# Modulation and first features of a hybrid attention layer: two hand-ordered stages replaced by one list schedule

## The chip, the cores and the metric

The kernel is one program on one core of a Trainium2 chip. The metric is the device time of one execution in microseconds (us). The engines are TensorE (PE in the profile, its weight loads PEld), VectorE (DVE), ScalarE (ACT), GpSimd (POOL) and SyncE (SP), which issues most DMAs.

## What is computed

One layer of a diffusion backbone: 512 latent and 256 context tokens, width 2048, two kinds of attention heads on one modulated input, one output projection, a gated MLP. The change concerns the first steps; the rest is named by its last lines:

```python
sc_, scc = jax.nn.silu(c), jax.nn.silu(c_ctx)                  # (1, 2048) each
mod_x = (sc_ @ w_ada[l] + b_ada[l])[:, None, :]                # six chunks of 2048
mod_c = (scc @ w_ada[l] + b_ada[l])[None, None, :]
sh1, s1, g1, sh2, s2, g2 = jnp.split(mod_x, N_MOD, axis=-1)
sh1c, s1c, ...           = jnp.split(mod_c, N_MOD, axis=-1)
h  = _modulate(_rmsnorm(x,  norm1_w[l]), sh1,  s1)             # h * (1 + scale) + shift
hc = _modulate(_rmsnorm(xc, norm1_w[l]), sh1c, s1c)
p  = h @ w_in                                                  # q, k, v, c_q, c_kv, k_rope
...
x = x + g1 * (_merge_heads(o_da, o_mla, ...) @ w_o[l])
h2 = _modulate(_rmsnorm(x, norm2_w[l]), sh2, s2)
x = x + g2 * _conv_ffn(h2, w_up[l], conv_w[l], conv_b[l], w_down[l])
return _rmsnorm(x, final_w)
```

## The kernel before

Everything is kept with features on the partitions: the 2048 model features are 16 tiles (index kt) of 128, each 512 latent columns (`a2k` tiles) and 256 context columns (two to a `c2k` tile). Products run on TensorE as three matmuls of split float32 numbers (helper `mm3`, L241 to L243): high x high, high x low, low x high, where ACT casts the high part and DVE subtracts it from the source to get the low part.

The program has five stages: modulation and first features; the other features and values; attention; output projection; MLP. The change rewrites the first.

**Head.** SP loads the rows `c` and `c_ctx`, then 16 tiles of x and 8 of ctx. ACT makes their silu; PE spreads each row over all partitions by matmuls with ones (L429), DVE copies `cb` and ACT copies `ccb` out of PSUM (L443, L445). ACT squares x (L435) and every other ctx tile (L437), DVE squares the other ctx tiles (L439) and adds all squares up (L441); PE sums over partitions (L448) and `rstd` makes the inverse norm (L297 to L302). GpSimd clears `cpad` and writes a DRAM tensor of zeros, `zero_d`, from it in pieces of 30 and of 18 floats (L333); attention reads it much later.

**Modulation of tile kt.** The scale needs 2048 products per feature for two vectors. For two tiles at once, `scales` loads four blocks `adak` of 512 KB, and PE multiplies them by `cpad` (which holds both silu vectors, 32 columns wide) in 16 matmuls per `products` call (L348, four for each block), accumulating into one PSUM bank `acc`; ACT copies the result (L350), PE sums it by `sel` (L352), DVE makes `a1` (L360). The shift reads a row block `ada` of 1 MB in two halves. For even kt DVE does it: four dot products of 1024 elements (L384; `modx` with `cb`, `modc` with `ccb`). For odd kt TensorE does it: 16 transposes in four batches (L400), each copied out by ACT (L401), then 16 products (L348) and a sum (L352).

**First features of tile kt.** DVE multiplies x by scale and inverse norm (L500, `h`), ACT adds the shift and rounds (L502), DVE makes the low part (L503); ACT and DVE split the weight block `w_g0` of 640 columns (L217, L218). PE then does five `mm3` of 512 columns and four of 256 into five latent and four context sums that stay in PSUM over all 16 tiles.

The head is written in the order wanted and kept by `manual_schedule`; from tile 0 on, `modulation(kt // 2 + 1)` is called ahead of every even kt and the framework's own scheduler orders the instructions by their place and by `high_priority`. Attention is ordered by a list scheduler in the kernel, class `Flow`: each step has an engine, a cost, a due time, and buffers taken from rings; a table `PLAN` shifts due times of parts, and `run` replays a queue per engine to fix the order. SP's loads are issued in order: one that waits for a free tile holds those behind it.

After the first stage `latent_norm` and `keys` read the sums out of PSUM, and ten more features follow, each with two weight blocks, while 48 more `ada` rows are multiplied by `cb` on DVE (helper `gemv`, L309).

Of the kernel before, what the change touches and what calls it, by code (L numbers as in the profile page):

```python
# [51 lines left out]
class Buf:  # L52


    def __init__(self, flow, ring, make):
        self.ring, self.make, self.tile = ring, make, None
        self.users, self.writers, self.readers, self.left = [], [], [], 0
# [7 lines left out]
class Step:  # L65
    __slots__ = ("eng", "cost", "lag", "at", "fn", "bufs", "left", "next", "takes", "start", "n", "ready")

    def __init__(self, eng, cost, lag, at, fn, n):
        self.eng, self.cost, self.lag, self.at, self.fn, self.n = eng, cost, lag, at, fn, n
        self.bufs, self.left, self.next, self.takes, self.ready = [], 0, [], [], 0.0  # L70
# [10 lines left out]


class Flow:
# [7 lines left out]
    def buf(self, make, ring=None, count=None):  # L91
        if ring and ring not in self.rings:
            self.rings[ring] = (count, [])
        return Buf(self, ring, make)

    def step(self, eng, cost, at, fn, r=(), w=(), needs=(), lag=None):
        at += self.plan.get(self.part, 0.0)
        s = Step(eng, cost, self.LAGS[eng] if lag is None else lag, at, fn, len(self.steps))
# [6 lines left out]
        for b in dict.fromkeys([*r, *w]):  # L105
            if b.ring and not b.users:
                s.takes.append(b)
            b.users.append(s)
            b.left += 1
            s.bufs.append(b)  # L110
# [10 lines left out]
    def run(self):  # L121
# [4 lines left out]
        engines = {"PE": -3.0, "ACT": 2.0, "DVE": 2.8, "POOL": 0.0, "SP": now, "X": -3.0}  # L126
# [6 lines left out]

        for s in self.steps:
            if not s.left:
                event(s.ready)
                open_[s.eng].append(s)
        order = []

        turns = {}  # L140
        for s in sorted(self.steps, key=lambda s: (s.at, s.n)):
            for b in s.takes:
                turns.setdefault(b.ring, []).append(b)

        def free(b):
            count, taken = self.rings[b.ring]
            if turns[b.ring][len(taken)] is not b:
                return False
            return len(taken) < count or taken[-count].left == 0

        event(now)
        for t in set(engines.values()):
            event(t)
        while events:
# [4 lines left out]
            for s in batch:  # L159
                if s is None:  # L160
                    continue
                for b in s.bufs:
                    b.left -= 1
                for n_ in s.next:
# [6 lines left out]
            for e in engines:  # L171
                while engines[e] <= now + 1e-9:
                    can = [s for s in open_[e] if s.ready <= now + 1e-9 and all(free(b) for b in s.takes)]
# [4 lines left out]
                    for b in s.takes:  # L178
                        self.rings[b.ring][1].append(b)
# [10 lines left out]
def layer_kernel(ctx: ExitStack, tc: tile.TileContext, small, rope, c_row, cc_row, x_t, ctx_t, ada, ada_k,  # L190
# [134 lines left out]


    zero_d = dram.tile([64, TT], F32, name="zero_d")
# [14 lines left out]
    def products(src, n):  # L342


        for j in range(4):
            for c in range(4):
                kt = 4 * j + c
                pe.matmul(acc[32 * c:32 * c + 32, :n], cpad[:, kt], src(kt), start=j == 0, stop=j == 3)  # L348
        row = st.tile([P, 2 * P], F32, tag="row", name=nm("row"), bufs=1)[:, :n]
        sc.copy(row, acc[:, :n])  # L350
        for i in range(n // P):
            pe.matmul(acc[:, 2 * i:2 * i + 2], row[:, i * P:(i + 1) * P], sel, start=True, stop=True)  # L352

    def scales(u, ws=None):

        ws = ws or columns(u)
        products(lambda kt: ws[kt // 4][:, kt % 4], 2 * P)
        for i in range(2):
            kt = 2 * u + i
            ve.tensor_scalar(out=a1[:, 2 * kt:2 * kt + 2], in0=acc[:, 2 * i:2 * i + 2], scalar1=b1[:, kt:kt + 1],  # L360
                             scalar2=col("n1", kt), op0=ALU.add, op1=ALU.mult)

    def columns(u):
        ws = []
        for j in range(4):
            wk = st.tile([P, 4, 2 * P], F32, tag="adak", name=nm("adak"), bufs=4)
# [91 lines left out]
    def modulation(u):  # L458
        if u:
            shifts(2 * u)  # L460
# [1397 lines left out]
```

## Time and profile before

| | us |
|---|---|
| median of three executions (2401.7 to 2403.73) | 2401.8 |
| the profiled execution, its own time | 2404.97 |
| its span in the trace | 2403.1 |
| PE busy in the span | 2342.3 (97%) |
| DVE busy | 1701.1 (71%) |
| ACT busy | 1153.6 (48%) |
| POOL busy | 336.3 (14%) |
| first matmul of the first features starts at | 49.30 |
| their last matmul starts at | 183.71 |

The trace gives, for each instruction, its start, its duration and what its engine waited for before it. Matmuls overlap, so the time that one takes on PE is the distance from its start to the next start, not its listed duration.

### The profile page before, as it was taken

The page shows a single profiled execution, that of the slowest core. Times are in us where ns is not written, and L with a number is a line of the kernel's source. Part 1 is how long each engine was busy: PE and PEld are TensorE (multiplying, and loading weights), DVE is VectorE, ACT ScalarE, POOL GpSimd, SP SyncE. Part 2 cuts the span into 40 slices and gives each one's busy share as a digit, 9 for nine tenths or more (in the row PEclk, how much of TensorE's full clock was granted, in tenths as well). Part 3 has the DMA queues.
Part 4 walks back from the last instruction along what each step waited for, and adds up shares of the span by engine and source line. Part 5 has one row for each costly group of instructions (what it writes and reads, how often), then busy time and mean ns, then how long its engine had stood idle before and what let it go on. Part 6 is the DMA issues. An engine that isn't in the chain of part 4 may idle for free.

```text
span 2403.1 us, 33008 instructions
## 1 busy us (share of the span) xinstructions
PE 2342.3 (97%) x12758; PEld 1981.3 (82%) x12758; DVE 1701.1 (71%) x2244; ACT 1153.6 (48%) x1752; POOL 336.3 (14%) x320
## 2 busy tenths in 40 slices
PE   5999999999999999999999999999999999999997
PEld 3678878887788888798888888888888888888887
DVE  6668886477878766399585757575767676766767
ACT  4333121177776732255454545454545444544546
POOL 0000000155433221100101010101010101111110
PEclk9999999999999999999999999999999999999999
DMA  8867899844521168333646465555554656565573
GB/s 281 295 230 277 304 336 330 269 130 139 156 64 50 34 255 320 131 115 97 144 130 144 128 144 137 140 140 141 132 147 123 153 122 158 123 153 128 140 186 105
DMA packets 132853, 404.31 MB, mean 168 GB/s; under 512 B 14628, under 2 KB 25380, under 8 KB 124244
## 3 DMA queue, kind: packets, MB, share of 16 engines
q1 hardware_dynamic: 106166, 351.66, 44.4%
q0 software_dynamic: 25376, 49.49, 11.9%
q8 instruction: 100, 1.64, 0.3%
q10 hardware_dynamic: 1152, 1.05, 0.1%
q14 instruction: 59, 0.48, 0.1%
HBM read 332.47 MB, written 69.67 MB: 167 GB/s over the span
## 4 chain that ended last, share of the span: by engine, by line
PE 84%; DVE 7%; DMA 4%; ACT 3%; issue 2%; SPq 0%; DVEq 0%; ACTq 0%
PE y L1577 12%; PE b L242 10%; PE b L241 10%; PE b L243 9%; PE z L1577 6%; PE y L1579 6%; PE s L241 3%; PE s L719 3%; PE s L243 3%; PE s L242 3%; PE z L1579 3%; DMA ada<-in_ada 3%; PE x L1577 2%; PE f L241 1%; PE f L242 1%
## 5 line engine op out<-in xcount | busy, mean ns | idle before, releaser
L1598 POOL DMA_DIRECT2D x_d<-xs x160 | 139.9, 1005 | 1161.4 <-ACT xs L1597 1159.5
L1433 DVE TENSOR_TENSOR wl<-wr,wh 128x1024 fp32r<-128x1024 f32 x144 | 176.5, 1225 | 158.6 <-ACT wh L1425 157.9
L1425 ACT CAST wh<-wr 128x1024 fp32r<-128x1024 f32 x144 | 151.1, 1049 | 234.8 <-PE b L242 120.7
L241 PE MATMUL b<-ah,wh 128*128 128x512 f32 (+1 forms) x664 | 256.8, 387 | 0.0
L242 PE MATMUL b<-al,wh 128*128 128x512 f32 (+1 forms) x664 | 256.7, 387 | 0.0
L243 PE MATMUL b<-ah,wl 128*128 128x512 f32 (+1 forms) x664 | 255.9, 385 | 0.0
L1433 DVE TENSOR_TENSOR wl<-rb,wh 128x1024 fp32r<-128x1024 f32 x123 | 150.0, 1220 | 126.8 <-ACT wh L1425 126.8
L1425 ACT CAST wh<-rb 128x1024 fp32r<-128x1024 f32 x123 | 129.3, 1051 | 186.5 <-PE b L242 115.8
L1433 DVE TENSOR_TENSOR wl<-ws,wh 128x1024 fp32r<-128x1024 f32 x123 | 150.1, 1221 | 89.8 <-ACT wh L1425 89.8
L1425 ACT CAST wh<-ws 128x1024 fp32r<-128x1024 f32 x123 | 128.3, 1043 | 130.1 <-PE b L242 45.2
L309 DVE CUSTOM_DVE_ANT_0 ada<-ada,cb,smt 128x2048 f32<-128x2048 f32 x64 | 152.3, 2383 | 46.6 <-DMA ada<-in_ada 46.6
L1577 PE MATMUL y<-a2k,wh 128*128 128x512 f32 x656 | 164.0, 392 | 0.0
L217 ACT CAST wh<-wr 128x1024 fp32r<-128x1024 f32 (+1 forms) x69 | 67.5, 978 | 195.2 <-PE s L243 48.8
L241 PE MATMUL b<-a2k,wh 128*128 128x512 f32 (+1 forms) x376 | 141.7, 377 | 5.9 <-ACT a2k L1282 4.3
L243 PEld LDWEIGHTS b<-ah,wl 128*128 128x128 f32 x664 | 124.8, 188 | 25.7
L241 PEld LDWEIGHTS b<-ah,wh 128*128 128x128 f32 x664 | 125.1, 188 | 22.9
L242 PEld LDWEIGHTS b<-al,wh 128*128 128x128 f32 x664 | 125.1, 188 | 22.0
L242 PE MATMUL b<-a2k,wh 128*128 128x512 f32 (+1 forms) x376 | 140.9, 375 | 0.0
L243 PE MATMUL b<-a2k,wl 128*128 128x512 f32 (+1 forms) x376 | 140.1, 373 | 0.0
L1577 PEld LDWEIGHTS y<-a2k,wh 128*128 128x128 f32 x656 | 118.6, 189 | 21.6
L218 DVE TENSOR_TENSOR wl<-wr,wh 128x1024 fp32r<-128x1024 f32 (+1 forms) x69 | 80.0, 1159 | 46.0 <-ACT wh L217 45.5
L722 DVE TENSOR_REDUCE m<-s 128x1 f32<-128x768 f32 x96 | 91.2, 951 | 28.0 <-PE s L719 27.5
(480 smaller groups left out, 5932.5 us busy)
## 6 DMA issues: line engine op xcount, KB each, us to landing
ada<-in_ada SPq DMA_DIRECT2D x64, 1024.0 KB, 7.0
rb<-in_w_up SPq DMA_DIRECT2D x123, 512.0 KB, 4.3
wr<-in_w_dn SPq DMA_DIRECT2D x88, 512.0 KB, 4.1
x_d<-xs POOLq DMA_DIRECT2D x160, 256.0 KB, 6.0
wr<-in_w_up SPq DMA_DIRECT2D x53, 512.0 KB, 4.2
wr<-in_w_f SPq DMA_DIRECT2D x34, 512.0 KB, 7.3
ada<-in_ada SPq DMA_DIRECT2D x32, 512.0 KB, 7.2
adak<-in_ada_k SPq DMA_DIRECT2D x32, 512.0 KB, 6.3
```

Source lines behind the costliest of these rows:

```text
L218: ve.tensor_tensor(dst_l, src, dst_h.bitcast(F32), op=ALU.subtract)
L241: pe.matmul(out, st[0], mv[0], start=start, stop=False, **kw)
L242: pe.matmul(out, st[0], mv[1], start=False, stop=False, **kw)
L243: pe.matmul(out, st[1], mv[0], start=False, stop=stop, **kw)
L309: ve.tensor_tensor_reduce(out=junk, in0=w, in1=vec, op0=ALU.mult, op1=ALU.add, scale=1.0, scalar=col("b_ada", j), accum_out=dst[:, j:j + 1])
L719: pe.matmul(s()[:, c0:c1], a, b[:, c0:c1], start=i == 0, stop=i == len(ms) - 1)
L722: step("DVE", 0.87, t + cost + 0.2, lambda: ve.tensor_reduce(out=m(), in_=s()[:, :TT], axis=AX.X, op=ALU.max, negate=True), r=[s], w=[m])
L1425: sc.copy(t, raw[:, k * n_:k * n_ + n_])
L1433: ve.tensor_tensor(t, raw[:, k * n_:k * n_ + n_], hi[k].bitcast(F32), op=ALU.subtract)
L1577: pe.matmul(o, w[j][0], hs[j], start=start and j == 0, stop=False, skip_group_check=True)
L1579: pe.matmul(o[:, h0], w[j][1], hs[j][:, h0], start=False, stop=j == 7, skip_group_check=True)
L1598: gp.dma_start(x1_d[dt], x, accum_op=ALU.add)
```

## The change

The first stage becomes part of a second `Flow`, and the `PLAN` table and the scheduler's rule for rings are replaced with it (a ring counts its live buffers instead of going round in turn, and a buffer taken early is not asked for again). This also reorders attention, whose code is otherwise the same.

Shifts: all tiles but 5 and 10 go to DVE, as dot products over a whole row of 2048 elements from one 1 MB load, 28 in place of 32 of half the length. Tiles 5 and 10 are turned on TensorE, with the products in two halves. The table of `ada` tiles in SBUF goes from five of 512 KB to three of 1 MB.

```diff
-        if kt % 2 == 0:
-            for i in range(2):
-                shift(kt, ws, i)
-            return
-        wt = st.tile([P, KT, P], F32, tag="wt", name=nm("wt"), bufs=1)
-        for q in range(4):
-            for i in range(4):
-                k = (q % 2) * 4 + i
-                pe.transpose(acc[:, i * P:(i + 1) * P], ws[q // 2][:, k * P:(k + 1) * P], ident)
-            sc.copy(wt[:, 4 * q:4 * q + 4].rearrange("p k f -> p (k f)"), acc)
-        products(lambda kt: wt[:, kt], P)
...
+    T0, PER = 31.0, 6.15
+    TURNED = (5, 10)
...
+            w = buf(lambda: st.tile([P, D], F32, tag="ada", name=nm("ada"), bufs=3), "ada", 3)
+            flow.part = f"lr{kt}"
+            load(T0 + PER * kt - 16 if kt else 16.9, 1060, lambda kt=kt, w=w: nc.sync.dma_start(w(), ada[kt]), [w])
...
+    def shift(kt):
+        if kt in TURNED:
+            turned_shift(kt)
+            return
+        w = rows[kt]
+        t = T0 + PER * kt - 10
+        for i in range(2):
+            at_b[i][kt] = b = buf(lambda: None)
+            d, vec = (modx, modc)[i][:, kt:kt + 1], (cb, ccb)[i]
+
+            def dot(d=d, vec=vec):
+                junk = st.tile([P, D], BF16, tag="junk", name=nm("junk"), bufs=1)
+                ve.tensor_tensor_reduce(out=junk, in0=w(), in1=vec, op0=ALU.mult, op1=ALU.add, scale=1.0,
+                                        scalar=col("b_ada", kt), accum_out=d)
+
+            flow.part = f"{'dp'[i]}{kt}"
+            step("DVE", 2.31, t + 2.6 * i, dot, r=[w, *wide[i]], w=[b], lag=0.2)
```

In the head, ACT now makes all squares and all copies of `cb` and `ccb`; the last two tiles' squares are not added on DVE but summed by PE (six matmuls of the sum over partitions in place of two); the inverse norm is made in two parts, latent and context.

```diff
-    for c0, c1, r in ((0, 480, slice(0, 64)), (480, TT, slice(64, P))):
-        gp.dma_start(zero_d[:, c0:c1].rearrange("p (k j) -> p k j", j=(c1 - c0) // KT),
-                     cpad[r, :, 2:2 + (c1 - c0) // KT])
...
+    z = kv.tile([P, TT], F32, tag="lt", name=nm("z"), bufs=3)[:64]
+    gp.memset(z, 0.0)
+    gp.dma_start(zero_d, z)
...
-            q = kv.tile([P, TT], F32, tag="nq", name=nm("nq"), bufs=1)
-            sc.square(q[:, :width], t)
...
+    for q, lat in zip(sq, lat0):
+        sc.square(q[:, :T], lat)
+    for t, lat in zip(ckv, lat0):
+        sc.copy(t[:, :T], lat)
```

So the zeros are written in the second stage, in whole rows, and the squares for the two latent norms are taken from PSUM ahead of the copies.

Three places in the order of the instructions. First TensorE in the middle of the stage, before, while an odd tile is turned (`ident` transposes of `ada`, products of `wt` with `cpad`; `b_332` to `s_426` are the feature sums):

```order
L243 MATMUL s_425<-a2k_1215,wl_986 128x512
L243 MATMUL b_332<-c2k_1213,wl_986 128x256
L241 MATMUL s_425<-a2k_1215,wh_985 128x512
L400 MATMUL b_334<-ident,ada_991 128x128 x4
L242 MATMUL s_425<-a2k_1216,wh_985 128x512
L243 MATMUL s_425<-a2k_1215,wl_986 128x512
L241 MATMUL b_332<-c2k_1213,wh_985 128x256
L242 MATMUL b_332<-c2k_1214,wh_985 128x256
L348 MATMUL b_334<-wt_993,cpad 32x128 x16
L243 MATMUL b_332<-c2k_1213,wl_986 128x256
L243 MATMUL s_426<-a2k_1215,wl_986 128x512
L242 MATMUL b_333<-c2k_1214,wh_985 128x256
```

The same engine in the changed program, between two tiles that are not turned (L252 to L254 are `mm3` now, L490 the scale products):

```order
L254 MATMUL b_475<-c2k_710,wl_589 128x256
L252 MATMUL s_450<-a2k_722,wh_692 128x512
L253 MATMUL s_450<-a2k_732,wh_692 128x512
L254 MATMUL s_450<-a2k_722,wl_708 128x512
L490 MATMUL b_346<-adak_756,cpad 32x256 x4
L490 MATMUL b_346<-adak_766,cpad 32x256 x4
L252 MATMUL b_475<-c2k_710,wh_579 128x256
L253 MATMUL b_475<-c2k_711,wh_579 128x256
L254 MATMUL b_475<-c2k_710,wl_589 128x256
L252 MATMUL b_457<-a2k_722,wh_692 128x512
```

Between the feature matmuls only the scale products are left; transposes stand there for two tiles instead of eight.

Second, VectorE in the middle of the stage, before (two weight blocks, then one even tile's four half dot products, each with its accumulator read; `modx`, `modc` without operands are those reads):

```order
L218 TENSOR_TENSOR wl_986<-wr_983,wh_985 128x640
L218 TENSOR_TENSOR wl_1038<-wr_1035,wh_1037 128x640
L384 ISA junk_1119,modx<-ada_1115,cb,smt 128x1024
L384 ISA modx 128x1
L384 ISA ada_1115,modc<-ada_1115,ccb,smt 128x1024
L384 ISA modc 128x1
L384 ISA junk_1121,modx<-ada_1117,cb,modx 128x1024
L384 ISA modx 128x1
L404 TENSOR_SCALAR modx<-b_334,smt 128x1
L404 TENSOR_SCALAR modc<-b_334,smt 128x1
```

And in the changed program (L557 the whole-row dot products, L581 and L586 the two passes over x):

```order
L557 ISA junk_964,modx<-ada_906,cb,smt 128x2048
L557 ISA modx 128x1
L581 SCALAR_TENSOR_TENSOR h_977<-a2k_232,a_91,rinv 128x512
L557 ISA junk_984,modc<-ada_906,ccb,smt 128x2048
L557 ISA modc 128x1
L586 SCALAR_TENSOR_TENSOR a2k_1008<-h_920,modx,a2k_979 128x512
L581 SCALAR_TENSOR_TENSOR h_920<-c2k_221,a_91,rinv 128x256
L557 ISA junk_1021,modc<-ada_966,ccb,smt 128x2048
L557 ISA modc 128x1
L478 TENSOR_TENSOR wl_1053<-wr_990,wh_1034 128x640
```

The dot products now stand singly between the passes over x of neighbouring tiles, twice as long each and for seven tiles of eight.

Third, SP at the end of the loads of x, before:

```order
L415 DMA a2k_205<-in_x_t 128x512
L418 DMA c2k_207<-in_ctx_t 128x512
L415 DMA a2k_209<-in_x_t 128x512
L375 DMA ada_211<-in_ada 128x1024
L375 DMA ada_213<-in_ada 128x1024
L367 DMA adak_215<-in_ada_k 128x1024
```

and in the changed program:

```order
L376 DMA a2k_257<-in_x_t 128x512
L463 DMA ada_263<-in_ada 128x2048
L463 DMA ada_278<-in_ada 128x2048
L463 DMA ada_290<-in_ada 128x2048
L376 DMA a2k_302<-in_x_t 128x512
L380 DMA c2k_307<-in_ctx_t 128x512
L376 DMA a2k_310<-in_x_t 128x512
```

Three whole `ada` rows (3 MB) moved ahead of the last two x tiles and the last ctx tile.

More of the change, by code (lines that the diff above doesn't have):

```diff
@@ L119, in step, with run @@
         return s
-    def run(self):
+    def run(self, begin):
         import heapq
         now = -100.0
-        engines = {"PE": -3.0, "ACT": 2.0, "DVE": 2.8, "POOL": 0.0, "SP": now, "X": -3.0}
+        engines = dict(begin)
         open_ = {e: [] for e in engines}
@@ L138, in run @@
         order = []
[L140 to L143, printed above, removed]
         def free(b):
[L146 to L153, printed above, removed]
+            return not b.ring or b.taken or turns[b.ring][0] is b and live[b.ring] < self.rings[b.ring]
         while events:
@@ L172, in run @@
                 while engines[e] <= now + 1e-9:
-                    can = [s for s in open_[e] if s.ready <= now + 1e-9 and all(free(b) for b in s.takes)]
+                    can = [s for s in open_[e] if s.ready <= now + 1e-9 and all(free(b) for b in s.bufs)]
                     if not can:
@@ L323, in layer_kernel @@
     st = tc.alloc_tile_pool(name="st", bufs=1, reuse_waits="tile")
-    zero_d = dram.tile([64, TT], F32, name="zero_d")
+    for i in range(4):
+        st.tile([P, 4, 2 * P], F32, tag="adak", name=nm("adak"), bufs=4)
+    st.tile([P, 640], F32, tag="wr", name=nm("wr"), bufs=2)
+    st.tile([P, D], F32, tag="ada", name=nm("ada"), bufs=3)
     cb = st.tile([P, D], F32, name="cb")
@@ L354, in scales @@
-    def scales(u, ws=None):
-        ws = ws or columns(u)
-        products(lambda kt: ws[kt // 4][:, kt % 4], 2 * P)
-        for i in range(2):
[L359 to L366, printed above, removed]
-            nc.sync.dma_start(wk, ada_k[u, j // 2][:, (j % 2) * 4:(j % 2) * 4 + 4])
-            ws.append(wk)
-        return ws
```

411 lines of the change are left out of this document (268 added, 143 removed), and 26 rows, old and new, of the table PLAN.

## The prediction

> **What bounds the kernel now.** I read the page first, then busy time in windows, the waits of PE in the first stage, and last its timeline start by start.
>
> ```profile
> PE 2342.3 (97%) x12758; PEld 1981.3 (82%) x12758; DVE 1701.1 (71%) x2244; ACT 1153.6 (48%) x1752; POOL 336.3 (14%) x320
> sum 200.00, PE 170.77 PEld 116.56 DVE 132.82 ACT 85.56 POOL 3.07; mean PE 8.54 PEld 5.83 DVE 6.64 ACT 4.28 POOL 0.15
> 100.00:110.00 10.00, 10.00 (x88) 8.10 (x88) 8.69 (x15) 5.27 (x10) 0.00 (x0) 1.00 0.71 244
> 110.00:120.00 10.00, 10.00 (x75) 6.56 (x74) 4.70 (x13) 2.85 (x5) 0.00 (x0) 1.00 0.99 358
> ...
> DMA packets 841, 1.54 MB, mean 384 GB/s; under 512 B 91, under 2 KB 91, under 8 KB 841
> ```
>
> The first row is the page's; the next three are windows (stretch, its length, busy time of PE, PEld, DVE, ACT, POOL, granted clock, DMA share, GB/s); the last is what the DMAs moved from 22 to 26 us. PE is idle for 2403.1 - 2342.3 = 60.8 us of the span, and 200 - 170.77 = 29.2 of that lies in the first 200 us, which the change rewrites. But in the middle of the stage PE is never idle, while DVE is idle 1.3 and 5.3 of 10 us and the DMAs move 244 to 358 GB/s, below the 384 they reached earlier. So two things can be had: PE's work in the middle, and the head, in which PE waits.
>
> ```profile
> PE s L448 <- DVE sqs L441: 14.0, 1, 14.0
> PE b L400 <- ACT wt L401: 1.4, 2, 0.7
> 49.30 1.22 PE L241 MATMUL s<-a2k,wh 128*128 128x512 f32 x2
> 183.71 0.39 PE L243 MATMUL b<-a2k,wl 128*128 128x512 f32 x1
> ```
>
> The waits (line, releaser, total us, times, longest) show the head's 14.0 us and little else. From the first feature matmul to the last start pass 134.4 us; with its 0.39 the stage ends at 184.1.
>
> **What is taken from PE.** Rows of PE's timeline (start, duration), one odd tile being turned and one block of scale products:
>
> ```profile
> 102.41 0.60 PE L400 MATMUL b<-ident,ada 128*128 128x128 f32 x4
> 102.76 0.48 PE L242 MATMUL b<-a2k,wh 128*128 128x512 f32 x1
> 103.08 0.39 PE L243 MATMUL b<-a2k,wl 128*128 128x512 f32 x1
> ...
> 107.72 1.08 PE L348 MATMUL b<-wt,cpad 128*32 128x128 f32 x32
> 108.73 0.39 PE L243 MATMUL b<-c2k,wl 128*128 128x256 f32 x1
> 108.95 0.39 PE L243 MATMUL s<-a2k,wl 128*128 128x512 f32 x1
> 109.18 0.28 PE L242 MATMUL b<-c2k,wh 128*128 128x256 f32 x1
> 109.30 0.32 PE L352 MATMUL b<-sel,row 128*128 128x2 f32 x2
> 109.48 0.37 PE L243 MATMUL b<-c2k,wl 128*128 128x256 f32 x1
> 109.69 0.40 PE L241 MATMUL s<-a2k,wh 128*128 128x512 f32 x1
> ...
> 114.22 0.64 PE L348 MATMUL b<-adak,cpad 128*32 128x256 f32 x8
> 114.79 0.39 PE L242 MATMUL b<-c2k,wh 128*128 128x256 f32 x1
> 115.02 0.28 PE L243 MATMUL b<-c2k,wl 128*128 128x256 f32 x1
> ...
> 119.39 0.60 PE L400 MATMUL b<-ident,ada 128*128 128x128 f32 x4
> ```
>
> Undisturbed, a matmul of 512 columns holds PE 0.23 us (108.95 to 109.18), one of 256 0.12 (109.18 to 109.30). A batch of four transposes takes 0.35 to the next start, and that next matmul 0.32 instead of 0.23: 0.44. The 16 products take 1.01 and delay their successor by 0.10: 1.11. The sum takes 0.18 + 0.09 = 0.27. A turned tile costs PE 4 x 0.44 + 1.11 + 0.27 = 3.1 us, and eight cost 25.1. Two tiles remain, their products in two halves (one more changeover, 0.1): 2 x 3.2 = 6.4. **PE is relieved of 18.7 us.** A block of scale products costs 0.57 + 0.11 = 0.68; in the new order three of the second pair's four blocks stand ahead of the first feature matmul, while PE waits there anyway: 2.0 us more. The period of a pair of tiles, 102.41 to 119.39, is 17.0 us, and 8 x 17.0 = 136 is the stage's 134.4: PE's queue is the stage.
>
> A page of the Trainium skill speaks against this reading. Trace Analysis, section Identifying the Most-Contended Engine, says that matmul busy time is not a good measure of the distance to the limit and sends one to the share of weight loads; here PEld is busy 8.10 and 6.56 of 10 us, so by that rule a quarter of PE's time would be free and the sum would lose its 18.7. No wait in the rows above bears that out; it stays below as a rival.
>
> **What is given to DVE.** Groups by shape (engine, operation, shapes, count, busy us, mean ns), of the first 185 us, and the half-row products beside the whole-row ones of the second stage:
>
> ```profile
> L503 DVE SCALAR_TENSOR_TENSOR a2k<-h,modx,a2k 128x512 fp32r<-128x512 f32 x16 | 12.0, 748 | 1.8 <-ACT a2k L502 1.8
> L503 DVE SCALAR_TENSOR_TENSOR c2k<-h,modc,c2k 128x256 fp32r<-128x256 f32 x16 | 7.7, 479 | 0.5 <-ACT c2k L502 0.5
> L500 DVE SCALAR_TENSOR_TENSOR h<-a2k,a,rinv 128x512 f32<-128x512 f32 x16 | 11.2, 745 | 0.0
> L500 DVE SCALAR_TENSOR_TENSOR h<-c2k,a,rinv 128x256 f32<-128x256 f32 x16 | 7.6, 479 | 0.0
> L218 DVE TENSOR_TENSOR wl<-wr,wh 128x640 fp32r<-128x640 f32 x16 | 13.2, 822 | 1.1 <-ACT wh L217 0.9
> L309 DVE CUSTOM_DVE_ANT_0 ada<-ada,cb,smt x24: 2331/2350/2356, 207.4 to 327.9; 128x2048 f32<-128x2048 f32 x24
>   DMA ada<-in_ada: 18.0, 13
> ```
>
> After its sums of squares DVE has 28 x 2.35 = 65.8 (dot products) + 12.0 + 7.7 + 11.2 + 7.6 + 13.2 = 117.5 us, and some 8 for the inverse norm, `a1` and accumulator reads, an estimate: **125 us** in one queue. It can begin when `cb` is spread and the first row is there. That is ACT's work:
>
> ```profile
> 10.27 0.63 ACT L435 ACTIVATE sqs<-a2k 128x512 f32<-128x512 f32 x1
> L435 ACT ACTIVATE sq<-a2k 128x512 f32<-128x512 f32 x15 | 9.4, 630 | 10.7 <-DVE sqs L441 5.4 <-DMA a2k<-in_x_t 5.2
> L437 ACT ACTIVATE sq<-c2k 128x256 f32<-128x256 f32 x8 | 3.2, 400 | 0.0
> L424 ACT ACTIVATE cb<-cb 1x2048 f32<-1x2048 f32 x1 | 1.9, 1892 | 0.0
> ```
>
> From 10.3: fourteen tiles of 0.63 + 0.40, two silus of 1.9, a table load (about 1.3) and four copies (some 0.55 each) come to 21.7, so `cb` is whole at 32.0. If x came earlier it could be some 4 us sooner, if x came late some 2 later. Then DVE's order has five dot products (11.8), one pass of the norm, a weight block (0.8), the rest of the norm (about 4) and one pass of x (0.75) ahead of the first feature matmul: 32.0 + 18.5 = 50.5, within 47 to 52. Today it starts at 49.3; I take **no change** there, +-2.
>
> DVE's end: 32 + 125 = 157 if it never waits. PE's end: 184.1 - 18.7 - 2.0 = 163.4. PE is later by 6 us, so PE still sets the end, but with DVE at over 90% in a fixed order. Behind a DVE instruction that waits stand the passes of the next tile, behind these PE, and SP's next weight loads. I add 2 us for such waits, between 0 (PE has lost its own waits on `wt`) and 10. **The stage ends at about 165, 19 us earlier.**
>
> **The rest.** The squares for the latent norms come straight from PSUM; PE waited for them and for the first weight block:
>
> ```profile
> PE s L577 <- ACT nq L575: 1.2, 2, 0.7
> PE b L241 <- ACT wh L217: 1.6, 1, 1.6
> PE po L242 <- DVE wtl L702: 4.3, 3, 1.8
> PE pt L739 <- DVE wtl L702: 1.9, 2, 1.5
> ```
>
> I take 1 us off the first two rows (the second stays: ACT casts the block after the keys, as now); bounds 0 and 2.8. In attention the last two rows hold nearly all of PE's waits. The reordering can win at most these 6.2 us and could lose as much; PE's instructions there are the same, so I take 0. In the second stage PE waits for little beside the first two rows, and the bytes to load are the same; the MLP is untouched. Both start earlier and keep their length.
>
> Sum: 19 + 1 = 20 us. The profiled execution took 2404.97 us, 3.2 above the median, its span 1.9 less; 2405 - 20 = 2385, against the median **2382**.
>
> **Rivals.**
>
> *The head shortens (0.15).* Loads are slow in the head's first half:
>
> ```profile
> DMA packets 257, 0.46 MB, mean 115 GB/s; under 512 B 35, under 2 KB 35, under 8 KB 257
> zero_d<-cpad POOLq DMA_DIRECT2D x1, 72.0 KB, 12.1
> ```
>
> The first row is 10 to 14 us; the second is GpSimd's second write of zeros, which lands 12.1 us after its issue near 2.7, so at about 14.8; by 22 us the rate is 384. Its pieces are 72 bytes, and the change takes them out of the head. Missing are about 1.1 MB in those 4 us, 2.9 us of loading at 384 GB/s, and before them perhaps as much again (an estimate). That ACT is bound by its own 21.7 limits the gain to about 5 us; with few waits after it, 2374. Against it: the write is only 72 KB, and a slow start of the reads themselves would look alike. By the Trainium skill, DMA: Bandwidth & Descriptors, section Specifications, transfers under 512 B are done by read and modify; the timing of the recovery agrees, and no run here separates the two yet.
>
> *DVE becomes the bound (0.13).* With waits of 0.75 us for each of 14 rows, as in the second stage (18.0 us over 24 rows), DVE ends at 157 + 10.5 = 168, and with the last tile's nine sums (5 x 3 x 0.23 + 4 x 3 x 0.12 = 4.9 us of PE) behind it the stage ends at 173: 2390.
>
> *Slower: rows arrive late (0.07).* Only three 1 MB tiles hold rows, a load waits for the second dot product of a row three back, and SP's queue stands behind it. DVE's lead over PE is 6 us, so with w us of waiting in each of 14 rows the stage grows by 14 w - 6. To lose the 20 us and 5 more w must pass (25 + 6) / 14 = 2.2 us, three times the 0.75 above. At 2.6 the time is 2412. For it: DMA must carry some 46 MB (16.8 each of rows and blocks, 6.3 of x and ctx, 5.2 of weights, small ones) in 160 us, 290 GB/s on average, pauses included; against it: it has carried 384.
>
> *No difference (0.05).* PE's row is full but holds slack that closes by itself when work is taken out: then only waits of about 3 us go, 2399. Against: the start distances of 0.23 and 0.12 stand between the changeovers without any gap. By the rule of the Trainium skill's Trace Analysis named above, this would be the likely case. That the change doesn't do what it says is excluded by the built order: two tiles are turned, 28 whole-row products stand on DVE.
>
> **Numbers.** Likeliest (0.60) is 2382, its own range 2374 to 2390. The range over all, leaving out the slower case and most of no difference, is 2369 to 2396. A measurement tells about 0.2% (4.8 us) from no change. Faster by more: 0.60 + 0.15 + 0.13 = 0.88; within: 0.05; slower: 0.07.
>
> **What would show it.** Right: 32 transposes instead of 128; first feature matmul at 47 to 52 and the last at about 165; PE back to back between, with waits on DVE under 5 us; 28 whole-row products of 2.35. If DVE waits for `ada` over 10 us, or PE on DVE over 8, one of the two middle rivals holds. A rate near 390 GB/s at 10 to 14 us shows the first. Wrong would be a first matmul after 55, or attention more than 6 us longer.

## The result, and the profile after

The changed kernel takes **2384.1 us** (median of four executions, 2378.5 to 2386.9) against 2401.9 before: a ratio of 0.9921, 95% interval 0.9903 to 0.994. The profiled execution took 2384.53 us against 2404.97, 20.4 less, with a span of 2382.5. Forecast were 2382 by the median and 20 us by the profiled executions.

The changed kernel's page, then its windows (stretch, its length, busy PE, PEld, DVE, ACT, POOL, granted clock, DMA share, GB/s), the groups of the first 185 us (x is the count) and the waits in that stage (us, times, longest):

```profile
PE 2322.1 (97%) x12470; PEld 1969.5 (83%) x12470; DVE 1720.8 (72%) x2216; ACT 1143.0 (48%) x1738; POOL 335.1 (14%) x320
```

```profile
10.00:20.00 10.00, 9.03 (x11) 3.77 (x12) 6.02 (x9) 9.76 (x18) 0.00 (x0) 1.00 1.06 413
100.00:110.00 10.00, 8.51 (x61) 6.21 (x60) 8.74 (x16) 2.56 (x5) 0.00 (x0) 0.83 0.94 373
130.00:140.00 10.00, 10.00 (x65) 6.92 (x64) 10.00 (x15) 3.19 (x5) 0.00 (x0) 1.00 1.00 379
```

```profile
L557 DVE CUSTOM_DVE_ANT_0 junk<-ada,cb,smt 128x2048 bf16<-128x2048 f32 x14 | 32.9, 2348 | 0.4 <-DMA ada<-in_ada 0.3
L557 DVE CUSTOM_DVE_ANT_0 junk<-ada,ccb,smt 128x2048 bf16<-128x2048 f32 x14 | 32.8, 2346 | 1.8 <-ACT ccb L404 1.8
...
L519 PE MATMUL b<-ident,ada 128*128 128x128 f32 x32 | 4.8, 272 | 0.0
```

```profile
PE b L490 <- DMA adak<-in_ada_k: 1.5, 1, 1.5
DVE junk L557 <- DMA ada<-in_ada: 0.3, 1, 0.3
```

PE lost 20.2 us of busy time and the span 20.6. The 32 transposes and 28 dot products of 2.35 us are those of two turned tiles and fourteen on DVE. From 130 to 140 us PE is as full as it was before, and DVE is now full too; PE's only wait between the first feature matmul and the last, 1.5 us for one scale block, lies in the window from 100 to 110. DVE waits 0.3 us for rows. The timeline gives the ends of the stage: the first feature matmul, the last, and the first weight block of the second stage.

```profile
51.60 0.79 PE L252 MATMUL s<-a2k,wh 128*128 128x512 f32 x1
...
160.48 0.28 PE L254 MATMUL b<-c2k,wl 128*128 128x256 f32 x1
160.60 2.31 PE L706 MATMUL s<-nq,ones 128*128 128x512 f32 x6
163.16 0.50 PE L252 MATMUL b<-a2k,wh 128*128 128x512 f32 x1 [0.24 <-ACT wh L228]
```

| profiled execution, us | before | after | moved | forecast |
|---|---|---|---|---|
| first feature matmul | 49.3 | 51.6 | +2.3 | 0, within 2 |
| from there to the stage's end | 134.8 | 109.2 | -25.6 | -18.7 |
| end of the stage | 184.1 | 160.8 | -23.3 | -19 |
| first weight block of the second stage | 187.7 | 163.2 | -24.6 | -20 |
| first matmul of the MLP | 1021.4 | 1002.2 | -19.2 | -20 |
| its own time | 2404.97 | 2384.53 | -20.4 | -20 |

So the sum is right and its terms are not: the feature stretch gave more than was priced, the head gave 2.3 back, and 5.4 us were lost between the second stage and the MLP. The head after, row by row, with what each waited for:

```profile
26.15 2.34 DVE L557 CUSTOM_DVE_ANT_0 junk<-ada,cb,smt 128x2048 bf16<-128x2048 f32 x1
...
26.29 2.93 PE L430 MATMUL s<-h,ones 128*128 128x512 f32 x4 [4.72 <-DVE h L426]
...
29.15 3.78 PE L397 MATMUL s<-ccb,ones 1*128 1x512 f32 x4
...
32.96 1.07 ACT L404 COPY ccb<-s 128x512 f32<-128x512 f32 x2 [6.93 <-PE s L397]
...
34.88 0.66 ACT L421 ACTIVATE h<-a2k 128x512 f32<-128x512 f32 x1
...
35.59 5.49 PE L430 MATMUL s<-h,ones 128*128 128x512 f32 x8 [2.67 <-ACT h L421]
...
41.12 0.69 DVE L443 TENSOR_SCALAR h<-s 128x512 f32<-128x512 f32 x1 [3.71 <-PE s L430]
...
48.88 2.79 PE L490 MATMUL b<-adak,cpad 128*32 128x256 f32 x24 [3.96 <-DVE a L504]
```

DVE's first dot product starts at 26.15, 6 us sooner than forecast, and still the first feature matmul isn't earlier. PE holds the last two spread matmuls of `ccb` (29.15) behind the first part of the sum over partitions (26.29), which waits for DVE's sums of squares. ACT therefore waits 6.93 us to copy `ccb`, and in ACT's fixed order the squares of the last two tiles (34.88) stand behind these copies; PE's sum over partitions waits for the squares, and DVE's inverse norm for the sum.

### The profile page after: what moved, and what is told of

Read it like the earlier page. It is cut to its first block, busy times and chain, and to the rows that moved or that the text cites. A ratio compares the mean times of both kernels' runs of the same rounds, so it can differ in the third digit from the quotient of the medians.

```text
span 2382.5 us, 32359 instructions
## 1 busy us (share of the span) xinstructions
PE 2322.1 (97%) x12470; PEld 1969.5 (83%) x12470; DVE 1720.8 (72%) x2216; ACT 1143.0 (48%) x1738; POOL 335.1 (14%) x320
## 4 chain that ended last, share of the span: by engine, by line
PE 87%; DVE 5%; DMA 3%; ACT 3%; issue 1%; SPq 0%; DVEq 0%; ACTq 0%
PE y L1715 13%; PE b L252 10%; PE b L253 10%; PE b L254 10%; PE z L1715 6%; PE y L1717 6%; PE s L252 4%; PE s L254 3%; PE s L253 3%; PE s L855 3%; PE z L1717 3%; PE x L1715 2%; PE f L252 1%; PE pt L875 1%; PE f L253 1%; PE f L254 1%
## 5 line engine op out<-in xcount | busy, mean ns | idle before, releaser
L1736 POOL DMA_DIRECT2D x_d<-xs x160 | 139.9, 1010 | 1161.2 <-ACT xs L1735 1159.1
L1563 ACT CAST wh<-wr 128x1024 fp32r<-128x1024 f32 x144 | 151.0, 1049 | 231.6 <-PE b L253 120.3
L252 PE MATMUL b<-ah,wh 128*128 128x512 f32 (+1 forms) x664 | 256.8, 387 | 0.0
L254 PE MATMUL b<-ah,wl 128*128 128x512 f32 (+1 forms) x664 | 255.9, 385 | 0.0
L252 PE MATMUL b<-a2k,wh 128*128 128x512 f32 (+1 forms) x376 | 141.9, 377 | 4.8 <-ACT a2k L1420 4.3
L254 PEld LDWEIGHTS b<-ah,wl 128*128 128x128 f32 x664 | 124.8, 188 | 25.7
L252 PEld LDWEIGHTS b<-ah,wh 128*128 128x128 f32 x664 | 125.1, 188 | 22.9
L228 ACT CAST wh<-wr 128x1024 fp32r<-128x1024 f32 x53 | 55.7, 1052 | 176.9 <-DMA wr<-in_w_o 49.7
L254 PE MATMUL b<-a2k,wl 128*128 128x512 f32 (+1 forms) x376 | 139.4, 372 | 0.3 <-DVE wl L229 0.3
L860 ACT ACTIVATE p<-s,m 128x768 f32<-128x768 f32 x96 | 86.8, 904 | 44.3 <-DVE m L858 41.0
```

The source lines that it names most:

```text
L252: pe.matmul(out, st[0], mv[0], start=start, stop=False, **kw)
L254: pe.matmul(out, st[1], mv[0], start=False, stop=stop, **kw)
L860: step("ACT", 0.9, t + cost + 1.2, lambda: sc.activation(p(), s()[:, :TT], AF.Exp, bias=m(), accum_out=lcol()), r=[s, m], w=[p, l], lag=0.25)
L1563: sc.copy(t, raw[:, k * n_:k * n_ + n_])
L1736: gp.dma_start(x1_d[dt], x, accum_op=ALU.add)
```

## The experiments

All times are medians, each with its ratio to the kernel before on the same chip and the 95% interval.

### Zeros written late, in the kernel before

```diff
-    for c0, c1, r in ((0, 480, slice(0, 64)), (480, TT, slice(64, P))):
-        gp.dma_start(zero_d[:, c0:c1].rearrange("p (k j) -> p k j", j=(c1 - c0) // KT),
-                     cpad[r, :, 2:2 + (c1 - c0) // KT])
...
     nc.sync.dma_start(cb, silu_c.to_broadcast([P, D]))
+    zero_d = dram.tile([64, TT], F32, name="zero_d")
+    z = kv.tile([P, TT], F32, tag="lt", name=nm("z"), bufs=3)[:64]
+    gp.memset(z, 0.0)
+    gp.dma_start(zero_d, z)
```

> The kernel before, with nothing changed but the zeros: written in whole rows in the second stage. Theory (the small-piece write holds back the loads): ACT's first square of x starts at about 6 us instead of 10.3, the rate from 10 to 14 us is near 390 GB/s instead of 115, the first feature matmul comes 3 to 4.5 us earlier than 49.3, and the time falls by 3 to 4.5 us, to about 2398. Rival (the loads start slowly by themselves): first square at 10.3 and 2402, no change. Second rival (the loads come earlier, but ACT's own work or a later wait sets the start): first square near 6, first feature matmul still at 49, 2402.

2399.1 us, ratio 0.9984 (0.9975 to 0.9992). What the DMAs moved from 10 to 14 us, and from the timeline the first feature matmul:

```profile
DMA packets 889, 1.62 MB, mean 406 GB/s; under 512 B 97, under 2 KB 97, under 8 KB 889
```

```profile
44.65 1.22 PE L241 MATMUL s<-a2k,wh 128*128 128x512 f32 x2
```

406 GB/s instead of 115, and a start 4.65 us earlier, at 44.65: the theory holds. One mark of it was wrong: ACT's first square stays at 10.1, since ACT's silus stand ahead of it.

### Zeros in the head, but in whole rows, in the kernel before

```diff
-    for c0, c1, r in ((0, 480, slice(0, 64)), (480, TT, slice(64, P))):
-        gp.dma_start(zero_d[:, c0:c1].rearrange("p (k j) -> p k j", j=(c1 - c0) // KT),
-                     cpad[r, :, 2:2 + (c1 - c0) // KT])
+    z = st.tile([P, 1, TT], F32, name="z")[:64]
+    gp.memset(z, 0.0)
+    gp.dma_start(zero_d.rearrange("p (k j) -> p k j", k=1), z)
```

> The kernel before with the zeros still written in the head, at the same place of GpSimd's queue, but from a tile of 64 whole rows of 768 floats instead of pieces of 30 and 18. Theory (the small pieces hold back the loads): 10 to 14 us run near 406 GB/s instead of 115, the first feature matmul comes near 44.7 as in the kernel with the zeros written late, and the time is about 2399. Rival (any write from GpSimd's queue in the head holds the loads back, whatever its pieces): 115 GB/s, 49.3 and 2402.

2398.7 us, 0.9983 (0.9972 to 0.9994), 405 GB/s from 10 to 14 us, first feature matmul at 43.21. The same tensor, queue and place cost nothing in rows of 3072 bytes: it is the pieces of 72 and 120 bytes.

### The head's order mended

After the list schedule two moves are made in its result, all else in its place:

```diff
-        flow.run({"PE": 1.0, "ACT": 3.8, "DVE": 5.0, "POOL": 2.0, "SP": 1.0, "X": 0.0})
+        flow.run({"PE": 1.0, "ACT": 3.8, "DVE": 5.0, "POOL": 2.0, "SP": 1.0, "X": 0.0},
+                 [(ccb_spread, ssq_sums), (last_squares, ccb_copies)])
```

Each pair names steps and the steps that they are put ahead of, in their engine's queue.

> The changed kernel with two moves: on TensorE the last two spread matmuls of ccb stand ahead of the sum over partitions, on ACT the squares of the last two tiles ahead of the copies of ccb. Theory (the earlier loads of the head were lost to this order): ACT's wait of 6.9 us goes, the sum over partitions ends near 33 instead of 41.1, the first feature matmul comes at 45 to 46.5 instead of 51.6, TensorE then runs as before, and the time falls by 5 to 6 us to about 2378.5. Rival (VectorE's queue or the rows set the end of the stage): the first matmul moves, but TensorE waits later, and the time falls by less than 2 us. Second rival (another wait in the head takes over, for a scale block or a row): the first matmul stays after 49.

2378.0 us, 0.9898 (0.9881 to 0.9914). The first feature matmul comes at 45.66, 5.9 us earlier, and the first weight block of the second stage at 157.33, 5.8 earlier: nearly all of the head's gain reaches the stage's end. The theory holds, and the wait for `ccb` was what ate the earlier loads. That the gain lasts to the end rests on the medians, 6.1 us: the profiled execution, 2387.5, was the slowest of the six, and between the first weight block of the second stage and the MLP it took 8.1 us more than the changed kernel's, 3.3 of it more waiting and 5.1 a lower clock.

### The old order of attention

```diff
-    flow = Flow(PLAN)
+    flow = OldFlow(OLD_PLAN)
...
-        flow.run({"PE": -3.0, "ACT": 2.0, "DVE": 2.8, "POOL": 0.0, "SP": -100.0, "X": -3.0})
+        flow.run()
```

Class and table are those of the kernel before, and used for attention alone.

> The changed kernel with the old table and the old ring rule for attention alone; the first stage is the changed one. Theory (4 us of the first stage's gain are given back by the new order of attention, in TensorE's waits of 1.5 and 2.2 us at the output projection): both waits go, the lead of 24.6 us over the kernel before, reached at the first weight block of the second stage, holds to the end, and the time is about 2380. Rival (the lead shrinks because everything comes earlier, with loads or rows that don't, whatever the order): the waits stay and the time is 2384. Second rival: the old order loses something that the new one had won, and the time is above 2385.

2374.9 us, 0.9891 (0.9877 to 0.9905). PE's waits from 660 to 1010 us, first of the changed kernel, then of this one (the 4.3 us are the norm ahead of the MLP, in both):

```profile
PE b L252 <- ACT a2k L1420: 4.3, 1, 4.3
PE s L254 <- DVE wl L229: 2.4, 2, 2.2
PE s L254 <- DVE wl L819: 1.5, 1, 1.5
PE po L253 <- DVE wtl L838: 0.4, 1, 0.4
```

```profile
PE b L389 <- ACT a2k L1557: 4.3, 1, 4.3
PE f L389 <- DVE rt L1094: 0.3, 1, 0.3
PE s L389 <- ACT p L997: 0.2, 1, 0.2
PE s L1765 <- ACT sq L1736: 0.2, 1, 0.2
```

The waits of 1.5 and 2.2 us are gone; the new order had put them there. By the medians it is worth 9 us, by the ratios 0.0030 of 2402, 7 us, with intervals that leave 2 to 13 us: more than the 3.7 us of the two waits, and the rest isn't settled. In this trace the second stage begins at 160.8, 2.4 us sooner than in the changed kernel's, with the same first stage.

### Both together

The two edits above in one kernel:

```diff
-        flow.run({"PE": 1.0, "ACT": 3.8, "DVE": 5.0, "POOL": 2.0, "SP": 1.0, "X": 0.0})
+        flow.run({"PE": 1.0, "ACT": 3.8, "DVE": 5.0, "POOL": 2.0, "SP": 1.0, "X": 0.0},
+                 [(ccb_spread, ssq_sums), (last_squares, ccb_copies)])
...
-    flow = Flow(PLAN)
+    flow = OldFlow(OLD_PLAN)
```

> The changed kernel with the two moves in the head and the old order of attention together. Theory (two separate losses, in different stages): they add, first feature matmul near 45.7, the first weight block of the second stage near 157.3, no wait of 1.5 or 2.2 us at the output projection, and the time is 2384.1 - 5.5 - 7 = about 2371.5. Rival (what is won early is lost again where rows come late, at the norm of the second latent near 317 us, at which both kernels waited 3 us or more): 2375 or above.

**2367.8 us**, 0.9851 (0.9838 to 0.9863): faster than both kernels, 34 us under the one before. First feature matmul at 46.10, first weight block of the second stage at 158.16. The two losses were separate, and what mending them gives adds up: 16 to 17 us together, 13 to 15 one by one (by the medians and by the ratios), the same within the intervals.

### Only the tiles moved, in the kernel before

```diff
-        if kt % 2 == 0:
+        if kt not in (5, 10):
```

> The kernel before with one line changed: all tiles but 5 and 10 are taken by VectorE, in half rows, in the framework's own order. If TensorE's queue alone is the stage, six turned tiles fewer give 18.7 us: 2383. Rival (VectorE becomes the bound without the new order and whole rows): a pair of tiles had 11.4 us of VectorE's work in a period of 17.0, in which it also waited 5.3 us for the scale; 5.1 us more for every odd tile (four half rows of 1.28) make 16.5 and leave nothing for that wait, so that the period stays near 17, TensorE waits on VectorE for 15 us or more, and the time is 2396 to 2405.

2399.2 us, 0.9982 (0.9973 to 0.9991). The window is the feature stretch, then PE's largest waits in it:

```profile
46.15:180.50 134.35, 121.69 (x784) 84.76 (x784) 113.39 (x207) 36.66 (x69) 0.00 (x0) 0.93 0.73 259
```

```profile
PE s L241 <- ACT a2k L502: 13.4, 6, 5.4
PE s L242 <- DVE a2k L503: 1.8, 5, 0.7
```

PE is relieved (121.7 us busy instead of 132.9) and the stretch is as long as before, 134.35 against 134.8. PE is idle for 12.7 us of it instead of 1.9, behind the passes over x on ACT and DVE (the longest wait of the first row, 5.4, ends with the first feature matmul and lies ahead of the stretch). By windows of 1 us another 9.0 us are lost to a lower granted clock, 2.6 before. So the rival holds, and the clock is a second price, which it didn't name. Most of what the time fell by is the earlier start, 46.15 instead of 49.30: tile 1 is no longer turned ahead of the first features. The move without the order brings nothing in the stretch.

### Dot products in two halves

```diff
-                ve.tensor_tensor_reduce(out=junk, in0=w(), in1=vec, op0=ALU.mult, op1=ALU.add, scale=1.0,
-                                        scalar=col("b_ada", kt), accum_out=d)
+                for hf in range(2):
+                    o = slice(hf * D // 2, (hf + 1) * D // 2)
+                    ve.tensor_tensor_reduce(out=junk[:, o], in0=w()[:, o], in1=vec[:, o], op0=ALU.mult, op1=ALU.add,
+                                            scale=1.0, scalar=d if hf else col("b_ada", kt), accum_out=d)
```

> The changed kernel with each dot product in two halves of 1024 elements, the order otherwise the same: 28 x (2 x 1.28 - 2.35) = 5.9 us more on VectorE, nothing more on TensorE. Theory (VectorE runs a few us ahead of TensorE): most of it is hidden, the stage ends 0 to 3 us later, 2384 to 2387. Rival (VectorE has no lead, its fixed order already paces TensorE tile by tile): the stage ends 6 us later and TensorE waits on VectorE, 2390. Second rival (the whole rows are what makes the move pay): the time comes back towards the 2399 of the kernel in which only the tiles were moved.

2386.5 us, 0.993 (0.9917 to 0.9943). The window from 50 to 160 us, of this kernel:

```profile
50.00:160.00 110.00, 108.27 (x786) 82.32 (x779) 107.26 (x193) 38.46 (x71) 1.48 (x2) 0.99 0.81 303
```

DVE is busy 107.3 of 110 us, 5.5 more than in the changed kernel, and the second stage begins at 162.2, no later than there. DVE's lead took all of it: the theory holds, and whole rows alone are not what pays.

### No tile turned, and six tiles turned

```diff
-    TURNED = (5, 10)
+    TURNED = ()
```

```diff
-    TURNED = (5, 10)
+    TURNED = (5, 7, 10, 11, 12, 14)
```

> The changed kernel with no tile turned: TensorE loses 2 x 3.2 = 6.4 us more, VectorE gets 4 x 2.35 = 9.4 more. Theory (TensorE sets the end, but VectorE, whose last instruction of the stage is at 157.2, is only a few us behind): VectorE ends near 166.5, the last tile's sums stand behind it, the first weight block of the second stage comes at 170 to 172 instead of 163.2, TensorE waits on VectorE within the stage for over 10 us, and the time is 2390 to 2394. Rival (VectorE has slack enough): the stage ends 6 us earlier, 2378.

> The changed kernel with tiles 5, 7, 10, 11, 12 and 14 turned, four more: TensorE gets 4 x 3.2 = 12.8 us, VectorE loses 18.8. Theory (TensorE's queue is the stage, at 3.1 to 3.2 us for a turned tile): the feature stretch grows from 109.2 to 122 us and the time to about 2397. Rival (a turned tile really costs TensorE 3.8 to 4.3 us, as the whole difference of 25.6 us between the stretches of the two kernels over six tiles would say): stretch 124.5 to 126.5, 2399 to 2401. Second rival (VectorE paces the stage): stretch unchanged or shorter, 2384 or less.

None turned: 2400.8 us, 0.9992 (0.9982 to 1.0003). Six turned: 2426.1, 1.0098 (1.0083 to 1.0113). Both are far beyond what was expected, and neither gives a price. With none turned the second stage begins at 180.1, 17 us later than in the changed kernel, and a window shows more than DVE's work:

```profile
130.00:150.00 20.00, 13.70 (x56) 10.71 (x53) 16.42 (x23) 5.24 (x9) 0.00 (x0) 0.59 0.69 252
```

PE and DVE both have gaps there, and the granted clock falls to 0.59. With six turned DVE waits for PE and ACT:

```profile
DVE modx L541 <- PE b L536: 20.7, 4, 9.6
DVE wl L478 <- ACT wh L477: 16.9, 6, 8.4
```

The number of turned tiles changes the list schedule of the whole stage, and the table has shifts made for tiles 5 and 10. That the table is why both are slow is argued, not shown. That VectorE has slack for two tiles more is refuted under this table; what a turned tile costs had to be asked in another way, with the order kept.

### Float32 matmuls put between the feature products

```diff
                 mm3(lat0(f), w, hx[kt], kt == 0, kt == KT - 1)
+                if 0 < kt < KT - 1 and f in (1, 3):
+                    for _ in range(1):
+                        pe.matmul(lat0(f)[0:30, 0:P], cpad[:, 0, 2:32], ident, start=False, stop=False,
+                                  skip_group_check=True)
```

and the same with `range(4)`.

> The changed kernel with one float32 matmul (30 x 128, zero weights, added into an open feature sum, so that nothing changes in it) put between two mm3 at 28 places of the first features. Theory (a changeover between the split matmuls and float32 ones costs TensorE on both sides, some 0.13 us ahead and 0.09 behind, beside 0.06 for the matmul): 28 x 0.28 = 7.9 us, the feature stretch grows from 109.2 to 117, 2392. Rival (only the follower is delayed, as the prediction counted): 28 x 0.15 = 4.2 us, 2388. Second rival (TensorE has slack between the tiles): under 2 us.

> The same with four such matmuls at each of the 28 places. Theory (changeover on both sides 0.22 us, matmul 0.06): 28 x 0.47 = 13.2 us, stretch 122.4, 2397; the difference to the kernel with one each is 28 x 3 x 0.06 = 5.3 us. Rival (0.09 for the changeover): 28 x 0.34 = 9.5 us, 2393.5. Second rival (slack): less than half of these.

With one each 2396.9 us, 0.9979 (0.9969 to 0.9989); with four 2412.9, 1.0044 (1.0031 to 1.0058). The stretch is read from the first feature matmul to the latent norm's first sum, of the kernel with one and then with four:

```profile
49.59 0.50 PE L252 MATMUL s<-a2k,wh 128*128 128x512 f32 x1
...
167.90 2.31 PE L710 MATMUL s<-nq,ones 128*128 128x512 f32 x6
```

```profile
50.99 0.80 PE L252 MATMUL s<-a2k,wh 128*128 128x512 f32 x1
...
188.35 2.31 PE L710 MATMUL s<-nq,ones 128*128 128x512 f32 x6
```

118.3 and 137.4 us, against 109.0 in the changed kernel. To compare them, windows of 1 us are summed over each stretch, and PE's idle time and the clock not granted are taken off: 104.2 in the changed kernel (1.5 idle and 3.3 of clock off), 118.0 with one, 136.0 with four, and 130.2 in the kernel before (1.9 and 2.6 off). So three more matmuls at 28 places cost 18.0 us, 0.21 each, and a place with one costs 13.8 / 28 = 0.49: **0.28 us for the changeover**, on both sides together, where the prediction counted 0.09 to 0.11. Start distances around the added matmuls agree: 0.09 ahead of them, 0.11 behind, and the first of a block takes 0.11 more than each further one. In another trace of the same first stage, that with the old attention, the cleaned stretch is 105.7; by it the changeover would be 0.23. The theory of two sides holds, a little larger than it said. Both times were missed, 2392 and 2397 expected, because a single float32 matmul with 30 columns of weights takes 0.21 and not 0.06. The 0.06 came from groups of four that stand in four column strips; that the strips make the difference isn't tested.

### Zeros in the head, in the changed kernel

```diff
+    zero_d = dram.tile([64, TT], F32, name="zero_d")
+    for c0, c1, r in ((0, 480, slice(0, 64)), (480, TT, slice(64, P))):
+        gp.dma_start(zero_d[:, c0:c1].rearrange("p (k j) -> p k j", j=(c1 - c0) // KT),
+                     cpad[r, :, 2:2 + (c1 - c0) // KT])
...
-    zero_d = dram.tile([64, TT], F32, name="zero_d")
-    z = kv.tile([P, TT], F32, tag="lt", name=nm("z"), bufs=3)[:64]
-    gp.memset(z, 0.0)
-    gp.dma_start(zero_d, z)
```

> The changed kernel with the zeros written in the head in small pieces, as before. Theory (in the changed head the sums of squares are bound by the loads): about 2.5 MB are late by 18 us, 6 us at 406 GB/s, the sums of squares end near 32 instead of 26.2, the first feature matmul comes at 55 to 57.5 instead of 51.6, and the time is 2388 to 2390. Rival (TensorE's and ACT's order in the head, which waits 6.9 us for the spread of ccb, hides the late loads): first matmul before 53.5 and the time under 2386.

2406.5 us, 1.0014 (1.0002 to 1.0027), where 2388 to 2390 was expected. The whole time says little: attention then waits once where the changed kernel doesn't.

```profile
56.50 0.50 PE L252 MATMUL s<-a2k,wh 128*128 128x512 f32 x1
...
164.04 0.50 PE L252 MATMUL b<-a2k,wh 128*128 128x512 f32 x1 [0.24 <-ACT wh L228]
...
475.04 0.77 PE L855 MATMUL s<-ks,qs 128*128 128x512 f32 x1 [15.14 <-DMA klz<-k_d]
```

The last row is a by-effect of the edit: with one tile fewer in the ring `lt`, the first load of `klz` is issued at 459.7 instead of 418.8. That the memory of those tiles is what it waits for is argued from the edit, not shown. The first stage can be read: the start is 4.9 us later, as expected, but the stage ends only 0.9 later, since PE's wait for a scale block (1.5) and the clock lost behind it fall away. So 4.9 us at the start were worth 0.9 at the stage's end here, while the mended head kept 5.8 of its 5.9: what a start is worth hangs on whether PE then waits for a block, which these two don't settle.

## Why the prediction was right, and which terms were not

- **What bounds the stage: right.** PE's queue was the stage. Without idle time and lost clock the stretch is 130.2 us before and 104.2 after; in the kernel in which PE was relieved without a new order, waits and a lower clock filled the room. By the rule of the Trainium skill (Perfetto Trace Analysis, Identifying the Most-Contended Engine) the weight loads' share would have left a quarter of PE free; this trace does not agree, as nothing but PE's own work ended the stage.
- **A turned tile at 3.1 us and 2.0 for the scale blocks: both mis-sized.** For the transposes the prediction priced a changeover by the delay of the follower alone, 0.09 us, and it left out that the changed order puts scale blocks side by side. Start distances, first of before, then of the changed kernel:

```profile
104.79 0.34 PE L242 MATMUL b<-c2k,wh 128*128 128x256 f32 x1
105.05 0.66 PE L400 MATMUL b<-ident,ada 128*128 128x128 f32 x4
105.46 0.36 PE L241 MATMUL b<-c2k,wh 128*128 128x256 f32 x1
105.67 0.39 PE L243 MATMUL s<-a2k,wl 128*128 128x512 f32 x1
```

```profile
81.87 0.40 PE L254 MATMUL s<-a2k,wl 128*128 128x512 f32 x1
82.19 1.93 PE L490 MATMUL b<-adak,cpad 128*32 128x256 f32 x32
84.06 0.50 PE L252 MATMUL s<-a2k,wh 128*128 128x512 f32 x1
84.39 0.39 PE L253 MATMUL s<-a2k,wh 128*128 128x512 f32 x1
```

  Before, the matmul of 256 columns ahead of this batch of transposes takes 0.26 instead of 0.12, the batch 0.41 instead of 0.35, and the matmul behind it 0.21 instead of 0.12. Not every batch has all of it: over 24 batches the delay ahead is 0 to 0.16, 0.06 on average; ahead of the products it is 0.09 to 0.16, ahead of the sums nothing. So a batch costs 0.53 on average, the products 1.25 and the sum 0.27, and a turned tile **3.6 us**. The prediction also counted all of tile 1, of which three batches, from 44.5 us on, stand ahead of the first feature matmul. With 29 batches, eight products and eight sums in the stretch before, and two turned tiles at 3.8 in two halves after, the turned tiles gave 27.7 - 7.6 = 20.1 us, not 18.7.

  A scale block that stands alone costs 0.10 ahead, 0.57 and 0.11 behind, 0.78 together; four side by side cost 0.09 + 1.87 + 0.10 = 2.06 instead of 3.12. Before, 28 blocks stand at 28 places of the stretch, in the changed kernel 25 at 14: 21.8 - 15.6 = 6.2 us, not 2.0. The two gains make 26.3, and the cleaned stretches differ by 26.0. These prices are averages of one trace each and no run tests them one by one. The kernel in which only the tiles were moved fits them less well: they give about 21 us for it, and its cleaned stretch of 112.7 is 17.5 shorter than before.
- **2 us for new waits: right in size.** 1.5 us for a block, none on DVE. But a wait has a second price, the clock (below): after this wait 1.7 us are lost to it. The other 1.6 of the stretch's 3.3 are lost at its start, as 2.6 were before.
- **DVE ends at 157: right by luck.** Its last pass starts at 157.2, but its dot products began 6 us sooner than forecast, and the path, priced without waits, held about 12 us of them, 3.7 for the sum over partitions. Its lead over PE is real: 5.5 us more went into it unseen. The rival in which DVE is the bound fell, and so did the one with late rows, which waited 0.3 us in all.
- **"No change" of the first matmul: a wrong reason.** It came at 51.6, within 47 to 52 but 2.3 later where +-2 was given. ACT's own 21.7 us did not set it. The small writes cost 4.65 us in the kernel before, so the first rival's mechanism was true; the rival fell because the new order of PE and ACT lost 5.9 us again.
- **1 us at the latent norm: right in size**, 1.3, from 23.3 at the end of the stage to 24.6 at the second stage's first weight block.
- **0 for attention: wrong.** 5.4 us were lost up to the MLP, 3.7 of them in two new waits. It lay within the bounds of 6.2, and with the 2.3 of the head it took back what the turned tiles and the scale blocks had given more: it is luck, errors that cancel, that the sum of 20 us came out.

## What to carry to other kernels

Price a changeover between kinds of matmuls on both sides, by the start distances ahead of it and behind it, and count the places: blocks that stand side by side pay it once. Whether moving work from a full engine to a half-empty one pays can hang on the order: here the move brought nothing to the stretch under the old order and nearly 26 us under a new one, and with the same table of shifts another split of the work lost all of it. After a new list schedule, look for a wait that blocks a fixed queue (an engine that copies behind a sum) and mend it by hand.

## What the runs showed of the hardware

**Small writes held back the loads.** Two writes, 0.2 MB together, in pieces of 72 and 120 bytes brought the loads to 115 GB/s from 10 to 14 us, against 406 without them and 405 with rows of 3072 bytes, and the first feature matmul back by 4.65 us or more. In those 4 us the 16 DMA engines count as 95% busy with packets of the loads' queue, so their busy share doesn't show it. The Trainium skill (DMA: Bandwidth & Descriptors, Specifications) says that transfers under 512 bytes are done by read and modify; the traces agree that they are the slow kind (8.7 and 12.1 us to landing, 5.7 in whole rows) and add that others pay, while the reading and modifying itself no run shows.

**After a short pause the clock can fall to half.** Windows of 1 us in the changed kernel, around PE's wait from 102.7 to 104.2:

```profile
103.00:104.00 1.00, 0.00 (x0) 0.00 (x0) 1.00 (x3) 0.00 (x0) 0.00 (x0) 1.00 1.01 393
...
105.00:106.00 1.00, 1.00 (x8) 0.87 (x7) 0.23 (x1) 1.00 (x3) 0.00 (x0) 0.98 1.00 418
106.00:107.00 1.00, 1.00 (x4) 0.81 (x4) 1.00 (x5) 0.14 (x1) 0.00 (x0) 0.50 1.07 434
...
108.00:109.00 1.00, 1.00 (x3) 0.77 (x3) 1.00 (x1) 0.00 (x0) 0.00 (x0) 0.50 0.92 386
109.00:110.00 1.00, 1.00 (x5) 0.80 (x4) 1.00 (x4) 0.66 (x1) 0.00 (x0) 0.81 1.04 423
...
900.00:910.00 10.00, 7.83 (x35) 6.13 (x34) 10.00 (x9) 5.27 (x7) 9.84 (x8) 1.00 0.82 297
```

From 106.0 to 109.4 PE runs at half its clock, 1.7 us lost beside the 1.5 us of waiting. It isn't so each time: 2.2 us at 904 (last row) were followed by none, nor was the wait of 1.3 us in the same stage of the kernel with the old attention. That the pause is the cause is read from what follows what; no run tests it. The Trainium skill (TensorE: Matmul & The Clock Gate, Part 1: The HAM clock gate) gives a free-running window of about 3.4 us, and half rate after an idle one; the 3.4 us of half clock agree, but here the pause ahead of it was 1.5 us, less than half such a window. At the second latent norm, whose code and order are the same in these kernels, PE waits 0.2 us in the changed kernel's trace and 3.6 in that with the old attention, where DVE had waited for rows; with the clock behind it that is a likely part of why executions of one kernel here differ by 8 us and more, though only single profiles show it.
